# Last feed-forward of a two-layer trunk kernel: high and low token parts in one 512-column operand, down-projection in one pass

## The chip, the cores and the metric

The kernel runs on one core of a Trainium2 chip. The metric is the device time of one execution in microseconds (us); the time of a kernel is the median of its runs. The trace is one execution taken by the hardware profiler. TensorE, VectorE, ScalarE, GpSimd and SyncE are called PE, DVE, ACT, POOL and SP, as in the profile; PEld is PE's weight load. Every engine takes its own instructions in program order and waits at one whose inputs are not there.

## The reference, cut to what matters

Two layers, each a SwiGLU feed-forward, three token mixers merged by gates, and a second SwiGLU feed-forward, on 256 latent tokens (`x`) and 256 context tokens. The context is not needed after the last mixer, so the last feed-forward works on 256 tokens. In float32:

```python
def _swiglu(h, w_up, w_down):
    u, v = jnp.split(h @ w_up, 2, axis=-1)
    return (jax.nn.silu(u) * v) @ w_down
...
x = x + 0.5 * mx[8] * _swiglu(_modulate(_rmsnorm(x, norm_g[l, 2]), mx[6], mx[7]), w_ffn2_in[l], w_ffn2_out[l])
...
return _rmsnorm(x, final_g)
```

The model width is 1024 (8 tiles of 128), the hidden width 2816 (22 tiles of 128).

## The kernel before, in words

**Products.** Activations lie feature-major, `xt[k]` being 128 features by tokens. A float32 product is made of three matmuls in the fp32r format: each operand is split into a high part (a copy rounded to fp32r, on ACT) and a low part (operand minus high part, on DVE; `split`, L127), and the kernel adds high weight x high token, low weight x high token and high weight x low token into the same PSUM columns. All matmuls are recorded at L110, all ScalarE activations at L119, all two-input VectorE operations at L122 and L125 (helpers `mm`, `act`, `tt`, `stt`).

**Units.** The weights come in units (`Unit`): one DMA of up to 512 KB (4 tiles of 128 rows by 256 columns) into a ring of 6 buffers `wr`, a split into a ring of 4 pairs `wh` and `wl`, and two parts, one for each 128 output columns (m = 0 and 1). `fm_units` (L411) makes the units of a product of 256 output columns; in one of 256 tokens a part issues 12 matmuls of 256 columns: for each of the 4 tiles high x high and low x high, then 4 times high weight x low token.

**Order of the work.** The program list is walked at L1372. For each part it issues the matmuls, then calls `ahead()` (L1347), which issues loads and splits as far as the rings allow, and then what takes the part's result from PSUM. A unit is split once the unit 4 places before it has had its last matmul issued. So behind an input unit pair the order on ACT and DVE is: result of m = 0, split of a later unit, result of m = 1, then the split that follows the next unit. There is one split for each unit and one result for each part of every second unit.

**The last feed-forward** is `ffn` (L487) with n = T = 256. It works in blocks of 256 hidden columns (2 tiles): 2 units of up weights, then 2 units of gate weights. For each tile, `up` (L496) takes Silu from PSUM on ACT; `gate` (L500) multiplies by the gate product from PSUM on DVE and splits the result into two tiles of the 69-slot ring, one instruction on ACT and one on DVE. `bounds = [0, 12, KF]` cuts the hidden tiles into two passes: 6 blocks, a down-projection over 12 tiles (4 column blocks x 3 units), then 5 blocks and a down-projection over 10 tiles (4 x 3 units, the third of 2 tiles). Each pass ends for each of the 8 output tiles in `residual` (L406), one DVE instruction that adds the gated result to `xt[m]`. After the last pass `to_out` (L1209) squares the tile on ACT, adds the square on DVE, scales on DVE and lets PE transpose the tile two places before; `final` (L1226) ends the kernel.

**Its start.** `across` (L455) puts the units of the first block aside (`far`): they are split into slots of the 69-slot ring instead of `wh` and `wl`, in two halves. The first is split before the norm, the second after it, the third and the fourth when their first part is reached. `norm` (L393) makes 8 scaled tiles on DVE, 8 high tiles `hh` on ACT, then 8 low tiles `hl` on DVE. The weights of the modulation's last term (`ada`, L280: two DVE instructions for each of 8 units) are mixed into the stage, 5 of them into blocks 2 and 3.

Of the kernel before, what the change touches and what calls it, by code (L numbers as in the profile page):

```python
# [10 lines left out]
F32R = mybir.dt.float32r  # L11
U32 = mybir.dt.uint32
ACTF = mybir.ActivationFunctionType
ALU = mybir.AluOpType
# [3 lines left out]
KD = 8  # L18
T = 256
FFN = 2816  # L20
KF = FFN // 128
# [69 lines left out]
def f32(ap):  # L91
    return ap.bitcast(F32)
# [3 lines left out]
def trunk_kernel(ctx: ExitStack, tc: tile.TileContext, a: dict, out: bass.AP, dbg=None):  # L96
# [8 lines left out]
    S = Ring(sp, N_SLOT, "s")  # L105
# [3 lines left out]
    def mm(o, l, r, start=True, stop=True):  # L109
        nc.tensor.matmul(o, l, r, start=start, stop=stop)  # L110
# [7 lines left out]
    def act(o, i, f, **kw):  # L118
        nc.scalar.activation(out=o, in_=i, func=f, **kw)  # L119

    def tt(o, x, y, op):
        nc.vector.tensor_tensor(out=o, in0=x, in1=y, op=op)  # L122

    def stt(o, x, s, y, op0, op1):
        nc.vector.scalar_tensor_tensor(out=o, in0=x, scalar=s, in1=y, op0=op0, op1=op1)  # L125

    def split(src, hi, lo):  # L127
        act(hi, src, ACTF.Copy)
        tt(lo, src, f32(hi), ALU.subtract)
# [24 lines left out]
    mods = [const.tile([128, 9, KD, 2], F32, name=f"mods{l}") for l in range(DEPTH)]  # L154
# [4 lines left out]
    xt = [None] * KD  # L159
    hh = [None] * KD  # L160
    hl = [None] * KD
# [204 lines left out]
    def scale_of(c):  # L366

        if c.start == 0:
            st["r"] = S.get()
        ps = P.get()  # L370
        mm(ps[:, c], ones_d, st["sq"][:, c])
        rstd_of(ps, c, st["r"])
        P.put(ps)

    def modulate(l, ni, ss, ks):

        todo = []
        for k, s in ((k, s) for k in ks for s in ss):
            c = slice(T * s, T * s + T)
            if s == 0:  # L380
                hh[k], hl[k] = S.get(F32R), S.get(F32R)
            t, shift = S.get(), mods[l][:, 3 * ni, k, s:s + 1]
            stt(t[:, c], xt[k][:, c], mods[l][:, 3 * ni + 1, k, s:s + 1], st["r"][:, c], ALU.mult, ALU.mult)
            act(hh[k][:, c], t[:, c], ACTF.Identity, bias=shift)
            todo.append((k, c, t, shift))
        for k, c, t, shift in todo:
            stt(hl[k][:, c], t[:, c], shift, f32(hh[k][:, c]), ALU.add, ALU.subtract)
            S.put(t)

    def norm_over():  # L390
        S.put(st["r"], st["sq"])

    def norm(l, ni, s, n):  # L393
        scale_of(slice(T * s, T * s + T))
        modulate(l, ni, (s,), range(KD))
        if T * s + T == n:
            norm_over()

    def drop_h():
        for k in range(KD):  # L400
            S.put(hh[k], hl[k])

    def wblock(w, r0, nk, c0, nc_):
        return w[r0:r0 + 128 * nk, c0:c0 + nc_].rearrange("(k p) c -> p k c", p=128)

    def residual(l, i, m, c, ps):  # L406
        for s in range(c.start // T, c.stop // T):
            cs = slice(T * s, T * s + T)
            stt(xt[m][:, cs], ps[:, cs], mods[l][:, i, m, s:s + 1], xt[m][:, cs], ALU.mult, ALU.add)

    def fm_units(w, c0, width, n, done, rh=None, kd=KD, r0=0, by_stream=False, turned=0):  # L411

        rh = rh or (lambda k: (hh[k], hl[k]))
        box = {}
        units = []
        nm = (width + 127) // 128
        cols_ = [slice(0, T), slice(T, n)] if by_stream and n > T else [slice(0, n)]  # L420
        for k0 in range(0, kd, 4):
            nk = min(4, kd - k0)

            def part(m, c, k0=k0, nk=nk):
                def go(u):
                    if k0 == 0 and c.start == 0:
                        box[m] = P.get()
                    ps = box[m]
                    cs = slice(128 * m, min(128 * m + 128, width))
                    o = ps[0:cs.stop - cs.start, c]  # L430
                    for k in range(nk):
                        h = rh(k0 + k)[0]
                        mm(o, u.hi[:, k, cs], h[:, c], k0 + k == 0, False)
                        mm(o, u.lo[:, k, cs], h[:, c], False, False)
                    for k in range(nk):
                        mm(o, u.hi[:, k, cs], rh(k0 + k)[1][:, c], False, k0 + k == kd - 1)

                    def out_():
                        if by_stream == "twice":
                            done(m, ps, c)  # L440
                        elif c.stop == n:
                            done(m, ps, slice(0, n))
                        if c.stop == n:
                            P.put(ps)

                    return k0 + nk == kd and out_
                return go

            u = Unit(wblock(w, r0 + 128 * k0, nk, c0, width), (nk, width), [part(m, c) for c in cols_ for m in range(nm)])
            u.cost = nk * nm * n  # L450
            u.turned = turned
            units.append(u)
        return units
# [33 lines left out]
    def ffn(l, w_in, w_out, n, gi, after, by_stream=True):  # L487

        first, units, last = [], [], []
        bounds = [0, 12, KF]  # L490
        for p0, p1 in zip(bounds, bounds[1:]):
            gs = {}
            for b in range(p0, p1, 2):
                sil = {}

                def up(m, ps, c, sil=sil):  # L496
                    sil[m] = S.get()
                    act(sil[m][:, c], ps[:, c], ACTF.Silu)

                def gate(m, ps, c, b=b, sil=sil, gs=gs):  # L500
                    s = sil.pop(m)
                    tt(s[:, c], s[:, c], ps[:, c], ALU.mult)
                    gs[b + m] = (S.get(F32R), S.get(F32R))
                    split(s[:, c], gs[b + m][0][:, c], gs[b + m][1][:, c])
                    S.put(s)

                us = fm_units(w_in[l], 128 * b, 256, n, up, by_stream=by_stream and b == 0)
                us += fm_units(w_in[l], FFN + 128 * b, 256, n, gate, by_stream=by_stream and b == 0)
                if b == 0:
                    first = us  # L510
                else:
                    units += us
            if p1 == KF:
                units += [drop_h, exp_ln_tables]
            for cb in range(0, KD, 2):
                end = p1 == KF and cb == KD - 2

                def down(m, ps, c, cb=cb, done=p1 == KF):
                    residual(l, gi, cb + m, c, ps)
                    if done:  # L520
                        after(cb + m, c)

                us = fm_units(
                    w_out[l], 128 * cb, 256, n, down, rh=lambda k, gs=gs, p0=p0: gs[p0 + k], kd=p1 - p0, r0=128 * p0,
                    by_stream=end and "twice",
                )
                if end:
                    last = us
                else:
                    units += us  # L530

            def free(gs=gs):
                for t in gs.values():
                    S.put(*t)

            if p1 < KF:
                units.append(free)
        return first, units, last, free
# [729 lines left out]
    up, gate, up2 = f1[0][0][0:2], f1[0][0][2:4], f1[0][1][0:2]  # L1268
    firsts = [up[0], gate[0], up2[0]]
    for u in firsts:  # L1270
# [4 lines left out]
    prog += early[7:13] + [("split", up[0]), lambda: scale_of(slice(0, 2 * T))] + early[13:]  # L1275
    prog += [
        lambda: modulate(0, 0, (0, 1), range(4)), ("split", gate[0]), ("split", up2[0]),
        up[0], *late[0:8], gate[0], *late[8:],
        lambda: modulate(0, 0, (0, 1), range(4, 8)), norm_over, up2[0], up[1], gate[1], up2[1],
    ]  # L1280
    prog += mixed(f1[0][1][2:], [side_loads] + ada_of(0, (2, 4, 3, 5, 7, 6, 8)))
    prog += across(f1[0][2], [f1[0][3]], lambda s: norm(0, 1, s, N2), mx[0][0], N2)
    prog += mx[0][1]
    prog += across(mx[0][2], [mx[0][3]], lambda s: norm(0, 2, s, N2), f2[0][0], N2)
    prog += mixed(f2[0][1], ada_of(1, (1, 0, 2, 4, 3, 5, 7)))
    prog += across(f2[0][2], [f2[0][3]], lambda s: norm(1, 0, s, N2), f1[1][0], N2)
    prog += mixed(f1[1][1], ada_of(1, (6,)))
    prog += across(f1[1][2], [f1[1][3]], lambda s: norm(1, 1, s, N2), mx[1][0], N2)
# [83 lines left out]
    for p in flat:  # L1372
# [5 lines left out]
        elif p[0] == "part":  # L1378
# [3 lines left out]
            u = p[1]  # L1382
            if u.far and u.hi is None:
                part(u)
            end = p[2](u)
# [58 lines left out]
```

## Time and profile before

| what | value |
|---|---|
| median of 3 runs | 2257.07 us (2256.82 to 2258.47) |
| the profiled execution's own time | 2259.09 us |
| its span, first to last instruction | 2257.3 us |
| PE busy | 2199.2 us (97%), 12903 matmuls |
| PEld busy | 1881.6 us (83%) |
| DVE busy | 1437.4 us (64%) |
| ACT busy | 933.2 us (41%) |
| POOL busy | 143.0 us (6%) |
| chain that ended last | PE 85%, DVE 8%, ACT 4%, issue 2%, DMA 1% |
| granted PE clock, mean | 0.989 of full |

Busy time counts an engine's instructions; matmuls are pipelined, so the start-to-start distance of matmuls is a better measure of PE's pace than their recorded durations, which overlap. "Idle before" tells what ended the idle time ahead of an instruction. The chain that ended last is followed back from the last instruction. The last feed-forward fills the stretch from 2044 to 2257 us.

### The profile page before, as it was taken

The page shows a single profiled execution, that of the slowest core. Times are in us where ns is not written, and L with a number is a line of the kernel's source. Part 1 is how long each engine was busy: PE and PEld are TensorE (multiplying, and loading weights), DVE is VectorE, ACT ScalarE, POOL GpSimd, SP SyncE. Part 2 cuts the span into 40 slices and gives each one's busy share as a digit, 9 for nine tenths or more (in the row PEclk, how much of TensorE's full clock was granted, in tenths as well). Part 3 has the DMA queues.
Part 4 walks back from the last instruction along what each step waited for, and adds up shares of the span by engine and source line. Part 5 has one row for each costly group of instructions (what it writes and reads, how often), then busy time and mean ns, then how long its engine had stood idle before and what let it go on. Part 6 is the DMA issues. An engine that isn't in the chain of part 4 may idle for free.

```text
span 2257.3 us, 32367 instructions
## 1 busy us (share of the span) xinstructions
PE 2199.2 (97%) x12903; PEld 1881.6 (83%) x12903; DVE 1437.4 (64%) x2428; ACT 933.2 (41%) x1565; POOL 143.0 (6%) x154
## 2 busy tenths in 40 slices
PE   7999999998999999999999999999999899998998
PEld 5888888976887788888888898888888688998998
DVE  5677788867465564677876565333358755867655
ACT  4321223455566545432223242222344457664443
POOL 0000000232100110000000000000004220100000
PEclk9999999999999999999999999999999999999999
DMA  8566565331222223355656535333233223356652
GB/s 311 163 189 187 186 190 182 114 87 57 66 66 66 66 59 100 120 163 184 193 182 194 168 118 153 98 98 94 89 95 105 88 75 113 113 167 201 216 183 94
DMA packets 246647, 304.49 MB, mean 135 GB/s; under 512 B 12874, under 2 KB 218180, under 8 KB 246496
## 3 DMA queue, kind: packets, MB, share of 16 engines
q1 hardware_dynamic: 245472, 301.65, 43.3%
q8 instruction: 101, 1.65, 0.3%
q10 hardware_dynamic: 448, 0.59, 0.1%
q14 instruction: 50, 0.41, 0.1%
q0 software_dynamic: 576, 0.18, 0.0%
HBM read 298.19 MB, written 4.19 MB: 134 GB/s over the span
## 4 chain that ended last, share of the span: by engine, by line
PE 85%; DVE 8%; ACT 4%; issue 2%; DMA 1%; SPq 0%; POOL 0%; ACTq 0%; DVEq 0%
PE p_t L110 84%; ACT s_t L119 3%; DVE wl L122 2%; DVE s_t L122 2%; DVE s_t L125 2%; PE p_t L696 1%; ACT wh L119 1%; DMA s_t<-in_w_ada_dram 1%; DVE av_s L754 1%; DVE s_t L761 0%; DVE cv_s L834 0%; SPq L185 0%; DVE s_t L955 0%; DVE av_s L755 0%; DVE s_t L976 0%
## 5 line engine op out<-in xcount | busy, mean ns | idle before, releaser
L110 PE MATMUL p_t<-s_t,wh 128*128 128x512 f32 (+1 forms) x6152 | 1640.3, 353 | 1.4 <-ACT wh L119 1.1
L110 PEld LDWEIGHTS p_t<-s_t,wh 128*128 128x128 f32 x6152 | 1087.6, 189 | 171.0 <-issue 9.4
L110 PE MATMUL p_t<-s_t,wl 128*128 128x512 f32 (+2 forms) x3076 | 1046.5, 352 | 2.9 <-DVE wl L122 2.9
L122 DVE TENSOR_TENSOR wl<-wr,wh 128x1024 fp32r<-128x1024 f32 (+2 forms) x423 | 498.1, 1184 | 507.6 <-ACT wh L119 507.4
L119 ACT ACTIVATE wh<-wr 128x1024 fp32r<-128x1024 f32 (+2 forms) x423 | 414.9, 988 | 643.4 <-PE p_t L110 290.3
L110 PEld LDWEIGHTS p_t<-s_t,wl 128*128 128x128 f32 (+1 forms) x3076 | 582.2, 189 | 81.5 <-DVE wl L122 3.4
L119 ACT ACTIVATE s_t<-s_t 128x512 fp32r<-128x512 f32 (+5 forms) x322 | 175.1, 544 | 340.3 <-DVE s_t L122 213.4
L110 PE MATMUL p_t<-s_t,s_t 128*128 128x256 f32 (+4 forms) x2040 | 275.1, 302 | 14.6 <-ACT s_t L119 10.4
L110 PEld LDWEIGHTS p_t<-s_t,s_t 128*128 128x128 f32 (+2 forms) x2040 | 231.9, 186 | 45.1 <-ACT s_t L119 14.4
L293 DVE SCALAR_TENSOR_TENSOR s_t<-wr,sc,s_t 128x512 f32<-128x512 f32 x392 | 268.9, 745 | 0.0
L119 ACT ACTIVATE s_t<-p_t 128x512 f32<-128x512 f32 (+5 forms) x344 | 171.9, 522 | 193.4 <-PE p_t L110 102.2
L122 DVE TENSOR_TENSOR s_t<-s_t,s_t 128x512 fp32r<-128x512 f32 (+3 forms) x217 | 128.8, 594 | 114.1 <-ACT s_t L119 113.1
L563 POOL TENSOR_TENSOR s_t<-s_t,s_t 128x256 f32<-128x256 f32 x26 | 22.0, 844 | 1384.9 <-DVE s_t L122 1371.1
L122 DVE TENSOR_TENSOR s_t<-s_t,p_t 128x512 f32<-128x512 f32 (+1 forms) x144 | 84.9, 590 | 26.4 <-PE p_t L110 19.4
L110 PE MATMUL p_t<-wh,s_t 128*128 128x512 f32 x256 | 83.1, 397 | 0.5 <-ACT wh L119 0.5
L125 DVE SCALAR_TENSOR_TENSOR s_t<-s_t,mods,s_t 128x256 fp32r<-128x256 f32 (+1 forms) x176 | 70.6, 478 | 10.3 <-ACT s_t L119 10.3
L125 DVE SCALAR_TENSOR_TENSOR s_t<-p_t,mods,s_t 128x256 f32<-128x256 f32 x136 | 61.0, 478 | 21.5 <-PE p_t L110 21.3
L110 PEld LDWEIGHTS p_t<-wh,s_t 128*128 128x128 f32 x256 | 48.9, 191 | 10.9 <-ACT wh L119 0.8
L122 DVE TENSOR_TENSOR s_t<-p_t,kf 32x256 f32<-32x256 f32 (+1 forms) x130 | 54.8, 421 | 3.5 <-PE p_t L110 1.4
L110 PE MATMUL p_t<-wl,s_t 128*128 128x512 f32 x128 | 51.0, 398 | 3.1 <-DVE wl L122 3.1
L119 ACT ACTIVATE s_t<-p_t,av_s 128x512 f32<-128x512 f32 (+1 forms) x48 | 29.2, 614 | 46.9 <-DVE av_s L755 46.9
L696 PE MATMUL p_t<-kf,s_t 128*128 128x128 f32 x240 | 36.2, 282 | 8.8 <-DVE s_t L122 4.1
(104 smaller groups left out, 803.3 us busy)
## 6 DMA issues: line engine op xcount, KB each, us to landing
wr<-in_w_ffn_in_dram SPq DMA_DIRECT2D x176, 512.0 KB, 4.4
wr<-in_w_ada_dram SPq DMA_DIRECT2D x128, 512.0 KB, 4.5
wr<-in_w_mix_in_dram SPq DMA_DIRECT2D x108, 512.0 KB, 3.7
wr<-in_w_ffn_out_dram SPq DMA_DIRECT2D x80, 512.0 KB, 3.7
s_t<-in_w_ada_dram SPq DMA_DIRECT2D x32, 256.0 KB, 6.2
wr<-in_w_mix_out_dram SPq DMA_DIRECT2D x16, 512.0 KB, 3.4
wr<-in_w_ffn_out_dram SPq DMA_DIRECT2D x16, 256.0 KB, 2.8
wr<-in_w_br_a_dram SPq DMA_DIRECT2D x8, 512.0 KB, 3.5
```

The lines of the kernel that those rows point to most:

```text
L110: nc.tensor.matmul(o, l, r, start=start, stop=stop)
L119: nc.scalar.activation(out=o, in_=i, func=f, **kw)
L122: nc.vector.tensor_tensor(out=o, in0=x, in1=y, op=op)
L125: nc.vector.scalar_tensor_tensor(out=o, in0=x, scalar=s, in1=y, op0=op0, op1=op1)
L293: eng.scalar_tensor_tensor(out=o, in0=x, scalar=c, in1=o, op0=ALU.mult, op1=ALU.add)
L563: nc.gpsimd.tensor_tensor(out=q[:, 0:T], in0=q[:, 0:T], in1=r[:, 0:T], op=ALU.subtract)
L696: nc.tensor.transpose(pt[:, 128 * t:128 * t + 128], p[:, 128 * t:128 * t + 128], ident)
L754: nc.vector.tensor_reduce(out=v[:, m:m + 1], in_=ps[m][:, 0:nk], axis=AX.X, op=ALU.max)
```

## The change

The low part of a token tile lies beside its high part, in columns 256 to 511 of the same slot (`modulate`, and `gs` in `gate`). In the last feed-forward (`wide`, n = T) a tile's three matmuls become two: high weight x (high | low token) with 512 columns, and low weight x high token with 256. The two halves of the PSUM bank are then summed where the result is taken: by a copy and an addition for up and gate, and by a second DVE instruction in `residual`. The hidden tiles are worked in one pass: 11 blocks, then a down-projection over 22 tiles, 4 column blocks of 6 units (the last of 2 tiles).

```diff
-    def modulate(l, ni, ss, ks):
+    def modulate(l, ni, ss, ks, beside=False):
...
-            if s == 0:
+            if s == 0 and beside:
+                hh[k] = S.get(F32R)
+                hl[k] = hh[k][:, T:2 * T]
+            elif s == 0:
                 hh[k], hl[k] = S.get(F32R), S.get(F32R)
...
-    def residual(l, i, m, c, ps):
+    def residual(l, i, m, c, ps, wide=False):
         for s in range(c.start // T, c.stop // T):
             cs = slice(T * s, T * s + T)
             stt(xt[m][:, cs], ps[:, cs], mods[l][:, i, m, s:s + 1], xt[m][:, cs], ALU.mult, ALU.add)
+            if wide:
+                stt(xt[m][:, cs], ps[:, T:2 * T], mods[l][:, i, m, s:s + 1], xt[m][:, cs], ALU.mult, ALU.add)
...
-                    for k in range(nk):
+                    if wide:
+                        for k in range(nk):
+                            h = rh(k0 + k)[0]
+                            mm(ps, u.hi[:, k, cs], h, k0 + k == 0, False)
+                            mm(ps[:, 0:T], u.lo[:, k, cs], h[:, 0:T], False, k0 + k == kd - 1)
+                    for k in range(0 if wide else nk):
                         h = rh(k0 + k)[0]
                         mm(o, u.hi[:, k, cs], h[:, c], k0 + k == 0, False)
                         mm(o, u.lo[:, k, cs], h[:, c], False, False)
-                    for k in range(nk):
+                    for k in range(0 if wide else nk):
                         mm(o, u.hi[:, k, cs], rh(k0 + k)[1][:, c], False, k0 + k == kd - 1)
...
-        bounds = [0, 12, KF]
+        wide = n == T
+        bounds = [0, KF] if wide else [0, 12, KF]
...
                     sil[m] = S.get()
-                    act(sil[m][:, c], ps[:, c], ACTF.Silu)
+                    if wide:
+                        act(sil[m][:, c], ps[:, c], ACTF.Copy)
+                        tt(sil[m][:, c], sil[m][:, c], ps[:, T:2 * T], ALU.add)
+                        act(sil[m][:, c], sil[m][:, c], ACTF.Silu)
+                    else:
+                        act(sil[m][:, c], ps[:, c], ACTF.Silu)
...
                     s = sil.pop(m)
-                    tt(s[:, c], s[:, c], ps[:, c], ALU.mult)
-                    gs[b + m] = (S.get(F32R), S.get(F32R))
+                    if wide:
+                        act(s[:, T:2 * T], ps[:, c], ACTF.Copy)
+                        tt(s[:, T:2 * T], s[:, T:2 * T], ps[:, T:2 * T], ALU.add)
+                        tt(s[:, c], s[:, c], s[:, T:2 * T], ALU.mult)
+                        g = S.get(F32R)
+                        gs[b + m] = (g, g[:, T:2 * T])
+                    else:
+                        tt(s[:, c], s[:, c], ps[:, c], ALU.mult)
+                        gs[b + m] = (S.get(F32R), S.get(F32R))
                     split(s[:, c], gs[b + m][0][:, c], gs[b + m][1][:, c])
```

## Rows read from the trace of the kernel before

**Rows 1.** Chain that ended last, 2060 to 2258 us: start us, us, what.
```profile
2061.05 170.21 PE p_t L110 x1425
...
2232.41 6.47 PE p_t L110 x54
```
**Rows 2.** Groups by line and shape, 2061 to 2246 us (busy, mean ns | idle before).
```profile
L122 DVE TENSOR_TENSOR wl<-wr,wh 128x1024 fp32r<-128x1024 f32 x58 | 70.9, 1224 | 56.0 <-ACT wh L119 56.0
L119 ACT ACTIVATE wh<-wr 128x1024 fp32r<-128x1024 f32 x58 | 61.1, 1053 | 48.3 <-PE p_t L110 33.0 <-issue 12.4 <-DMA wr<-in_w_ffn_in_dram 2.8
...
L119 ACT ACTIVATE s_t<-s_t 128x256 fp32r<-128x256 f32 x22 | 9.2, 417 | 37.2 <-DVE s_t L122 37.2
L122 DVE TENSOR_TENSOR s_t<-s_t,p_t 128x256 f32<-128x256 f32 x22 | 9.1, 414 | 1.6 <-PE p_t L110 1.6
...
L293 DVE SCALAR_TENSOR_TENSOR s_t<-wr,sc,s_t 128x512 f32<-128x512 f32 x10 | 7.0, 744 | 0.0
```
**Rows 3.** ACT in order of time, behind a block's gate units.
```profile
2114.11 1.04 ACT L119 ACTIVATE wh<-wr 128x1024 fp32r<-128x1024 f32 x1
2116.77 0.42 ACT L119 ACTIVATE s_t<-s_t 128x256 fp32r<-128x256 f32 x1 [1.62 <-DVE s_t L122]
2117.10 1.04 ACT L119 ACTIVATE wh<-wr 128x1024 fp32r<-128x1024 f32 x1
```
**Rows 4.** DVE in order of time, the same stretch.
```profile
2115.18 1.22 DVE L122 TENSOR_TENSOR wl<-wr,wh 128x1024 fp32r<-128x1024 f32 x1 [0.53 <-ACT wh L119]
2116.33 0.41 DVE L122 TENSOR_TENSOR s_t<-s_t,p_t 128x256 f32<-128x256 f32 x1
2117.22 0.42 DVE L122 TENSOR_TENSOR s_t<-s_t,s_t 128x256 fp32r<-128x256 f32 x1 [0.48 <-ACT s_t L119]
```
**Rows 5.** Chain that ended last, 1480 to 1620 us, matmuls of 512 columns.
```profile
1479.80 140.31 PE p_t L110 x619
```
**Rows 6.** DVE in order of time, two dependent operations in a row (mixer's end).
```profile
2021.18 0.41 DVE L122 TENSOR_TENSOR s_t<-s_t,p_t 128x256 f32<-128x256 f32 x1
...
2021.63 0.42 DVE L122 TENSOR_TENSOR s_t<-s_t,s_t 128x256 f32<-128x256 f32 x1
```
**Rows 7.** PE in order of time, start of the stage.
```profile
2049.53 2.08 PE L110 MATMUL p_t<-s_t,s_t 128*128 128x256 f32 x8 [4.88 <-ACT s_t L119]
2052.16 7.04 PE L110 MATMUL p_t<-s_t,s_t 128*128 128x256 f32 x40 [0.55 <-DVE s_t L125]
2060.19 0.38 PE L110 MATMUL p_t<-s_t,s_t 128*128 128x256 f32 x1 [0.99 <-ACT s_t L119]
2061.05 3.13 PE L110 MATMUL p_t<-s_t,s_t 128*128 128x256 f32 x23 [0.47 <-DVE s_t L122]
```
**Rows 8.** ACT in order of time, start of the stage.
```profile
2054.28 1.28 ACT L119 ACT_TABLE_LOAD   x1
2057.80 0.39 ACT L119 ACTIVATE s_t<-p_t 128x256 f32<-128x256 f32 x1 [2.23 <-PE p_t L110]
...
2059.24 0.38 ACT L119 ACTIVATE s_t<-p_t 128x256 f32<-128x256 f32 x1
2059.52 1.14 ACT L119 ACTIVATE s_t<-wr 128x512 fp32r<-128x512 f32 x2
```
**Rows 9.** Windows of 1 us: PE, PEld, DVE, ACT, POOL busy, PEclk, DMA share, GB/s.
```profile
2045.00:2046.00 1.00, 0.00 (x0) 0.00 (x0) 1.00 (x3) 0.58 (x2) 0.00 (x0) 0.89 0.14 20
...
2054.00:2055.00 1.00, 1.00 (x6) 1.00 (x6) 1.00 (x4) 0.98 (x2) 0.00 (x0) 0.50 0.00 0
...
2056.00:2057.00 1.00, 1.00 (x10) 1.00 (x9) 1.00 (x2) 0.00 (x0) 0.00 (x0) 0.99 0.00 0
...
2060.00:2061.00 1.00, 0.38 (x1) 0.19 (x1) 1.00 (x3) 1.00 (x3) 0.00 (x0) 1.00 0.87 299
```
**Rows 10.** Chain that ended last, the tail: start us, us, what.
```profile
2246.55 0.50 DVE s_t L125
```

More of the change, by code (lines that the diff above doesn't have):

```diff
@@ L394, in norm, with drop_h @@
         scale_of(slice(T * s, T * s + T))
-        modulate(l, ni, (s,), range(KD))
+        modulate(l, ni, (s,), range(KD), n == T)
         if T * s + T == n:
             norm_over()
-    def drop_h():
+    def drop_h(beside=False):
         for k in range(KD):
-            S.put(hh[k], hl[k])
+            S.put(hh[k])
+            if not beside:
+                S.put(hl[k])
     def wblock(w, r0, nk, c0, nc_):
         return w[r0:r0 + 128 * nk, c0:c0 + nc_].rearrange("(k p) c -> p k c", p=128)
-    def residual(l, i, m, c, ps):
+    def residual(l, i, m, c, ps, wide=False):
         for s in range(c.start // T, c.stop // T):
@@ L409, in residual, with fm_units @@
             stt(xt[m][:, cs], ps[:, cs], mods[l][:, i, m, s:s + 1], xt[m][:, cs], ALU.mult, ALU.add)
-    def fm_units(w, c0, width, n, done, rh=None, kd=KD, r0=0, by_stream=False, turned=0):
+            if wide:
+                stt(xt[m][:, cs], ps[:, T:2 * T], mods[l][:, i, m, s:s + 1], xt[m][:, cs], ALU.mult, ALU.add)
+    def fm_units(w, c0, width, n, done, rh=None, kd=KD, r0=0, by_stream=False, turned=0, wide=False):
         rh = rh or (lambda k: (hh[k], hl[k]))
@@ L497, in up @@
                     sil[m] = S.get()
-                    act(sil[m][:, c], ps[:, c], ACTF.Silu)
+                    if wide:
[4 more added lines that the diff above has]
+                        act(sil[m][:, c], ps[:, c], ACTF.Silu)
                 def gate(m, ps, c, b=b, sil=sil, gs=gs):
                     s = sil.pop(m)
-                    tt(s[:, c], s[:, c], ps[:, c], ALU.mult)
-                    gs[b + m] = (S.get(F32R), S.get(F32R))
+                    if wide:
[7 more added lines that the diff above has]
+                        gs[b + m] = (S.get(F32R), S.get(F32R))
                     split(s[:, c], gs[b + m][0][:, c], gs[b + m][1][:, c])
                     S.put(s)
-                us = fm_units(w_in[l], 128 * b, 256, n, up, by_stream=by_stream and b == 0)
-                us += fm_units(w_in[l], FFN + 128 * b, 256, n, gate, by_stream=by_stream and b == 0)
+                us = fm_units(w_in[l], 128 * b, 256, n, up, by_stream=by_stream and b == 0, wide=wide)
+                us += fm_units(w_in[l], FFN + 128 * b, 256, n, gate, by_stream=by_stream and b == 0, wide=wide)
                 if b == 0:
@@ L513, in ffn @@
             if p1 == KF:
-                units += [drop_h, exp_ln_tables]
+                units += [lambda: drop_h(wide), exp_ln_tables]
             for cb in range(0, KD, 2):
@@ L518, in down @@
                 def down(m, ps, c, cb=cb, done=p1 == KF):
-                    residual(l, gi, cb + m, c, ps)
+                    residual(l, gi, cb + m, c, ps, wide)
                     if done:
@@ L524, in ffn @@
                     w_out[l], 128 * cb, 256, n, down, rh=lambda k, gs=gs, p0=p0: gs[p0 + k], kd=p1 - p0, r0=128 * p0,
-                    by_stream=end and "twice",
+                    by_stream=end and "twice", wide=wide,
                 )
@@ L533, in free @@
                 for t in gs.values():
-                    S.put(*t)
+                    S.put(*t[0:1 if wide else 2])
             if p1 < KF:
```

## Prediction

> **What bounds the kernel now.** I read the chain that ended last, then the groups by line and shape, then the queues of ACT and DVE in order of time, and last the start and the tail. From 2061.05 the chain is 170 us of matmuls and nothing else [rows 1]: PE sets the pace, and 54 matmuls in 6.47 us make 0.1198 us each. Behind it the groups show ACT waiting 33.0 us for PE before weight splits [rows 2]: ACT has time to spare. But the same group view shows a second thing: in front of 22 high parts of the gated tiles ACT stood 37.2 us waiting for DVE, 1.7 each, and DVE stood 56 us waiting for ACT's `wh`. In time order the reason is seen. Behind a gate tile the two engines hand work back and forth and neither runs ahead: `wh` on ACT at 2114.11, `wl` on DVE at 2115.18, the product at 2116.33, its high part on ACT at 2116.77, the next `wh` at 2117.10 [rows 3, 4]. The round takes 1.07 + 1.15 + 0.44 + 0.33 = 2.99 us, and none of it waits for PE. Before the change only the two gate tiles of a block run it; the two up tiles' Silu is on ACT alone. A block of 4 units costs PE 96 x 0.1198 = 11.50 us, so it is covered.
>
> **The matmuls.** 44 up and gate tiles x 8 and 8 output tiles x 22 make 528 triples. A 512-column matmul in a stretch of nothing else takes 140.31 / 619 = 0.2267 us [rows 5]. A triple goes from 3 x 0.1198 = 0.3594 to 0.2267 + 0.1198 = 0.3465: 0.0129 saved, 6.8 us in all. No row shows the two shapes alternating. The bounds: nothing saved if the narrow one takes longer behind the wide one, 13 us if the overhead of both were gone; I take the two rows' sum, since both carry the same 13 ns over their streaming time (107 and 213 ns at 2.4 GHz). The Trainium skill (TensorE: Matmul & The Clock Gate, "Back-to-back issue gap") gives 262 and 518 cycles for 256 and 512 columns when warm, 109 and 216 ns; by it the triple would save 2.6 ns and the whole 1.4 us. The rows disagree, both being 11 ns longer, and the rows are used.
>
> **Taking results out.** An up tile now needs a copy on ACT, an addition on DVE, Silu on ACT. The copy (0.39, like the Silu from PSUM [rows 8]) lies under `wl`. The addition has the product's shape (414 ns [rows 2]) and Silu now reads the slot, like the high part (417). So an up tile runs the same round as a gate tile: 2.99 us where now Silu needs no DVE. A gate tile gets one more DVE operation that depends on the last; two such operations start 0.45 apart [rows 6], so its round is 3.44. Each of the four results of a block stands in program order behind one weight split, so a block costs the pair of engines 2 x 2.99 + 2 x 3.44 = 12.86 us, while PE needs 32 x 0.3465 = 11.09. **The pair becomes the bound**, by 1.77 us for each of the 10 blocks behind the first: 17.7 us. To it comes what else is in the two queues: 5 pairs of `ada` operations (744 ns each [rows 2], 1.4 us a pair); behind an up tile they lie under Silu and the next `wh`, behind a gate tile (2 of 5) they hold the next `wl` by 0.8, so 1.6; and the load of the exp/ln tables behind the last gate, 1.28. Against it stands the lead: a unit is split when PE finishes the unit 4 places before, in about 2.3 us (1.07 + 1.23), and used 3 units later, 3 x 2.77 = 8.3; 6.0 us of delay cost nothing. Loss: 17.7 + 1.6 + 1.3 - 6.0 = 14.6 us, all in PE's waits for `wl` from about the fourth block to the first units of the down-projection. There the splits come without results and cost DVE 1.2 us against 2.77 of PE, so PE is the bound again.
>
> **One pass.** The same 24 loads of the down weights, and the same 16 additions to `xt` (8 tiles x 2 halves instead of 8 x 2 passes), each under matmuls but the last. What moves: the 12 down units of the first pass, in which ACT and DVE catch up today, no longer stand between blocks 6 and 7, so the lead is not refilled. Fewer slots are held (22 instead of up to 24 for `gs`, 8 instead of 16 for `hh` and `hl`). The loads are released by splits in the same order on SP's queue; one wait of 2.8 us for a load exists now [rows 2].
>
> **The start.** PE begins at 2049.53 with high tiles alone and gets on at 2052.16 with the first low tile [rows 7]. The wide matmul needs both at once, so everything starts at 2052.16; `norm` issues the same instructions. The clock is at 1.2 GHz until 2056.0 [rows 9]: 5.8 triples at 0.66, then 6.2 at 0.3465, and the first up tile is done at 2058.3, where Silu started at 2057.80 [rows 8]. Then, in queue order: copy 0.41; the table load 1.28, which now stands ahead of the waiting Silu before PE is done [rows 8] and comes behind the copy, since a copy did not need it; Silu 0.33; ring `wh` and `wl` 1.07 + 1.15; the second tile's addition 0.44 and Silu 0.33; the halves of the third unit's weights, 0.66 and 0.73. PE is back in full stride at about 2064.7 against 2061.05 [rows 7]: +3.6. If the load stays ahead of the copy, 0.9 less.
>
> That leaves PE without matmuls for some 4.2 us from 2059.7. In the stop of 4.9 us before 2049.53 the clock fell to half and came back at 2056.0; in the stop of 1.9 us to 2061.05 it stayed at full [rows 7, 9]. The new stop is nearer to the longer one: I take a fall, about 5 us of dense matmuls at half speed, +2.5 (bounds 0 and 3.3, half of the 6.5 us between 2049.53 and 2056.0).
>
> **The tail.** Behind the last matmuls `residual` stands twice on the path (for tiles 6 and 7), each longer by one operation of 0.50 [rows 10] that depends on the one before: +1.0.
>
> **Sum**: -6.8 + 14.6 + 3.6 + 2.5 + 1.0 = +14.9 us, on 2259.09 for the profiled execution 2274.0; the median of the runs lies 2.0 below that execution, so **2272.0**.
>
> **Rivals.** (1) *The round keeps up.* Place: ACT and DVE in blocks 2 to 11. It decides at 11.09 us a block: if the copy and addition of an up tile overlapped the weight split, as Silu does now, a block would cost the pair some 10 us and PE would stay the bound. Then -6.8 + 3.6 + 1.0 = -2.2 us: 2254.9, and with a start that costs only 1 us 2252.3. For it: ACT is busy 41% and DVE 64% of the span. Against it: the queue is in order, and the four handoffs of the gate round are there in the rows with no gap that PE ends. Were the skill's pair of gaps right, the matmuls would save only 1.4 and this rival would give 2260. (2) *Loads run late*: `ada` units hold load buffers until DVE reaches them, now up to 10 us later; one landing of 4 to 5 us exposed once or twice more on the pair's path gives 2277 to 2280. For it, the one wait of 2.8 us today; against it, slower splits need loads less often. (3) *The wide pair saves nothing*: PE would need 11.50 a block, the pair still binds, 10 x 1.36 + 2.9 - 6.3 = 10.2 in place of 14.6 - 6.8: 2274; hardly told apart by time, but by the distance of matmuls.
>
> **How the numbers follow.** What a measurement of this kernel can tell from no change is about 0.2%, 4.5 us. The pair as the bound has 0.78, with loads late on top 0.10, the round keeping up 0.12, of which a third ends over 0.2% faster. Slower 0.88, same 0.08, faster 0.04. The range: rounds 0.2 us shorter (40 of them, -8) and no fall of the clock (-2.5) give 2261.5; 0.05 longer for two more handoffs in each round (+4) and a late load (+4) give 2280.
>
> **What would show it.** PE's idle time before matmuls with `wl` or `wh`, ended by DVE `wl`, now 0, should come to about 15 us, in waits of 0.4 to 0.9 each unit from the fourth block on; ACT should hold no waits for PE before `wh` in that stretch and wait for DVE before 44 Silu and high parts. Two matmuls of 512 and 256 columns should take 0.347 together. At the start PE should pass 2064 before full stride, with the table load behind the first copy. If PE's chain is unbroken from there to the tail, the forecast is wrong.

## The result, and the profile after

The changed kernel takes **2273.78 us** (median of 4 runs, 2273.48 to 2275.28); the kernel before, run beside it, 2257.77 (4 runs). The ratio is 1.0068, 95% interval 1.0055 to 1.0081: 16 us slower. The profiled execution took 2275.28 us, its span 2273.5, against 2259.09 and 2257.3 before.

The page's first and fourth part (busy us, share and instructions of each engine; chain by engine):

```profile
PE 2199.4 (97%) x12375; PEld 1853.8 (82%) x12375; DVE 1453.5 (64%) x2472; ACT 943.8 (42%) x1609; POOL 144.2 (6%) x154
...
PE 82%; DVE 10%; ACT 5%; issue 2%; DMA 1%; SPq 0%; POOL 0%; ACTq 0%; DVEq 0%
```

PE has 528 matmuls fewer (one for each *triple*: the three matmuls that one 128x128 tile of weights took before, now a pair of 512 and 256 columns) and is busy as long as before; DVE and ACT have 16 and 11 us more work. None of this tells 16 us of loss. The chain does: PE's share of it fell from 85% to 82%, and where it was 170 us of matmuls without a break [rows 1], it now reads (chain that ended last; start us, us, what):

```profile
2052.48 6.29 PE p_t L110 x24
...
2064.46 30.64 PE p_t L110 x159
...
2110.95 21.94 PE p_t L110 x120
2132.89 1.03 ACT wh L119
...
2135.86 1.05 ACT wh L119
2136.94 1.23 DVE wl L122
2138.53 0.43 DVE s_t L122
2139.31 1.05 ACT wh L119
...
2210.94 18.77 PE p_t L110 x107
```

PE sets the pace only where the chain shows it in long pieces. From 2132.89 to 2210.94 it is nearly all ACT and DVE, in the order `wh`, `wl`, addition, `wh`, though PE's first wait for them in this stretch comes only at 2167.43. ACT in order of time, one block of that stretch:

```profile
2135.86 1.04 ACT L119 ACTIVATE wh<-wr 128x1024 fp32r<-128x1024 f32 x1
2136.81 0.36 ACT L119 ACTIVATE s_t<-p_t 128x256 f32<-128x256 f32 x1
2138.99 0.42 ACT L119 ACTIVATE s_t<-s_t 128x256 fp32r<-128x256 f32 x1 [1.81 <-DVE s_t L122]
2139.31 1.04 ACT L119 ACTIVATE wh<-wr 128x1024 fp32r<-128x1024 f32 x1
...
2142.76 1.04 ACT L119 ACTIVATE wh<-wr 128x1024 fp32r<-128x1024 f32 x1
...
2145.43 0.42 ACT L119 ACTIVATE s_t<-s_t 128x256 f32<-128x256 f32 x1 [1.36 <-DVE s_t L122]
2145.75 1.04 ACT L119 ACTIVATE wh<-wr 128x1024 fp32r<-128x1024 f32 x1
...
2148.74 1.04 ACT L119 ACTIVATE wh<-wr 128x1024 fp32r<-128x1024 f32 x1
```

The distance from one `wh` to the next is the round: 3.45 us twice behind a gate tile, 2.99 twice behind an up tile, 12.88 for the block. ACT is idle for 1.81 and 1.36 us of each, and cannot use it: the `wh` of the next unit stands behind a Silu or a high part that waits for DVE, and DVE's next work, `wl`, waits for that `wh`. Neither is short of time: from 2133 to 2211 us ACT is busy for 41 and DVE for 47 of 78 us (window: PE, PEld, DVE, ACT, POOL busy, PEclk, DMA share, GB/s):

```profile
2133.00:2211.00 78.00, 73.73 (x402) 60.99 (x400) 47.35 (x72) 41.34 (x73) 0.00 (x0) 1.00 0.51 159
```

The groups from 2061 to 2262 us say it in sums (busy, mean ns | idle before):

```profile
L110 PEld LDWEIGHTS p_t<-s_t,wl 128*128 128x128 f32 x495 | 94.1, 190 | 7.6 <-DVE wl L122 7.5
...
L119 ACT ACTIVATE wh<-wr 128x1024 fp32r<-128x1024 f32 x59 | 61.6, 1046 | 11.2 <-PE p_t L110 8.5 <-issue 2.7
...
L119 ACT ACTIVATE s_t<-s_t 128x256 f32<-128x256 f32 x27 | 11.3, 418 | 43.3 <-DVE s_t L122 30.0 <-DVE s_t L125 13.2
...
L119 ACT ACTIVATE s_t<-s_t 128x256 fp32r<-128x256 f32 x22 | 9.2, 418 | 39.0 <-DVE s_t L122 39.0
```

ACT's wait for PE before `wh` fell from 33.0 us [rows 2] to 8.5, all in the down-projection (from 2064 to 2208 us it is 0.0); new is the wait of Silu for DVE. PE's own waits from 2040 to 2270 (us in total, times, longest; those of the tail and one of 1.5 us ahead of the stage left out):

```profile
PE p_t L110 <- DVE s_t L125: 7.5, 1, 7.5
PE p_t L110 <- ACT s_t L119: 4.3, 1, 4.3
PE p_t L110 <- DVE s_t L293: 4.1, 1, 4.1
PE p_t L110 <- DVE wl L122: 3.5, 8, 0.8
...
PE p_t L110 <- ACT wh L119: 0.8, 1, 0.8
```

The first is the wait for the norm (4.88 + 0.55 before, with 2.08 us of matmuls of high tiles between [rows 7], now in one piece), the second the new stop behind the first two units. The third is one that I had not listed: PE standing at the 16 `pick` matmuls of the `ada` sum (small matmuls that add up the last modulation term), which are in PE's queue, for a DVE operation that the rounds had delayed. PE in order of time there, and windows of 2 us around it (PE, PEld, DVE, ACT, POOL busy, PEclk, DMA share, GB/s):

```profile
2106.02 0.28 PE L110 MATMUL p_t<-s_t,wl 128*128 128x256 f32 x1
2110.38 1.20 PE L110 MATMUL p_t<-s_t,pick 128*32 128x128 f32 x16 [4.08 <-DVE s_t L293]
```
```profile
2110.00:2112.00 2.00, 1.47 (x17) 0.86 (x18) 1.90 (x3) 1.24 (x3) 0.00 (x0) 0.76 0.68 183
2112.00:2114.00 2.00, 2.00 (x7) 1.65 (x7) 1.41 (x4) 0.95 (x2) 0.00 (x0) 0.50 0.91 266
2114.00:2116.00 2.00, 2.00 (x12) 1.74 (x11) 1.55 (x2) 0.68 (x2) 0.00 (x0) 0.89 1.06 354
```

Behind the stop the granted clock stands at 0.50 (1.2 GHz) for about 3.4 us. The start, ACT in order of time, and a window:

```profile
2058.79 0.38 ACT L119 ACTIVATE s_t<-p_t 128x256 f32<-128x256 f32 x1 [4.15 <-PE p_t L110]
2059.19 1.28 ACT L119 ACT_TABLE_LOAD   x1
...
2063.47 0.42 ACT L119 ACTIVATE s_t<-s_t 128x256 f32<-128x256 f32 x1 [1.35 <-DVE s_t L122]
2063.79 1.14 ACT L119 ACTIVATE s_t<-wr 128x512 fp32r<-128x512 f32 x2
```
```profile
2064.00:2070.00 6.00, 5.54 (x16) 4.43 (x17) 3.72 (x5) 2.92 (x5) 0.00 (x0) 0.50 0.71 213
```

The table load stands behind the first copy, the third unit's halves come last, PE is back at 2064.46 and at half clock until 2070.0.

**Where 16 us went.** Start: 2064.46 for 2061.05, 3.4, of which 0.3 came from ahead of the stage (the norm's first matmuls stand at 2044.27 for 2043.95). Half clock on 5.54 us of matmuls: 2.8. Picks: a wait of 4.1, and 1.6 for the clock behind it (the shares missing in three windows of 2 us: 0.48 + 1.00 + 0.22, a little of it idle). Rounds: the 78.05 us from 2132.89 hold 200 triples, which take PE about 69.9 (88 up to 2163.8 at 0.3533, the others near 0.3467): 8.2. Of these, 2.1 are PE's waits for `wh` and `wl` at the first triple of the down-projection, whose split stands on ACT behind the load of the exp/ln tables (1.28 us from 2207.28). Tail: from PE's last product to the end 11.8 us for 10.8: 1.0. Matmuls: about 280 triples at 0.3467 instead of 0.3594, 230 at 0.3533: 5.0 saved. 3.4 + 2.8 + 5.7 + 8.2 + 1.0 - 5.0 = 16.1; the spans differ by 16.2.

### The profile page after: what moved, and what is told of

It reads as the page before. It is cut to its first block, busy times and chain, and to the rows that moved or that the text cites. A ratio compares the mean times of both kernels' runs of the same rounds, so it can differ in the third digit from the quotient of the medians.

```text
span 2273.5 us, 31401 instructions
## 1 busy us (share of the span) xinstructions
PE 2199.4 (97%) x12375; PEld 1853.8 (82%) x12375; DVE 1453.5 (64%) x2472; ACT 943.8 (42%) x1609; POOL 144.2 (6%) x154
## 4 chain that ended last, share of the span: by engine, by line
PE 82%; DVE 10%; ACT 5%; issue 2%; DMA 1%; SPq 0%; POOL 0%; ACTq 0%; DVEq 0%
PE p_t L110 80%; DVE wl L122 3%; DVE s_t L122 3%; ACT s_t L119 3%; ACT wh L119 2%; DVE s_t L125 2%; PE p_t L723 1%; DMA s_t<-in_w_ada_dram 1%; DVE av_s L781 1%; DVE s_t L788 0%; DVE s_t L293 0%; DVE cv_s L861 0%; SPq L185 0%; DVE s_t L982 0%; DVE av_s L782 0%
## 5 line engine op out<-in xcount | busy, mean ns | idle before, releaser
L110 PEld LDWEIGHTS p_t<-s_t,wh 128*128 128x128 f32 x5656 | 1025.5, 189 | 193.2 <-issue 9.4
L110 PE MATMUL p_t<-s_t,wl 128*128 128x512 f32 (+2 forms) x3076 | 1062.9, 352 | 6.4 <-DVE wl L122 6.4
L122 DVE TENSOR_TENSOR wl<-wr,wh 128x1024 fp32r<-128x1024 f32 (+2 forms) x423 | 498.0, 1185 | 498.8 <-ACT wh L119 498.3
L119 ACT ACTIVATE s_t<-s_t 128x512 fp32r<-128x512 f32 (+5 forms) x344 | 184.3, 536 | 380.9 <-DVE s_t L122 245.3
L119 ACT ACTIVATE s_t<-p_t 128x512 f32<-128x512 f32 (+5 forms) x366 | 179.8, 512 | 198.0 <-PE p_t L110 107.3
L122 DVE TENSOR_TENSOR s_t<-s_t,s_t 128x512 fp32r<-128x512 f32 (+3 forms) x217 | 128.9, 594 | 113.9 <-ACT s_t L119 112.9
L122 DVE TENSOR_TENSOR s_t<-s_t,p_t 128x512 f32<-128x512 f32 (+1 forms) x166 | 94.2, 567 | 30.0 <-PE p_t L110 17.9
L125 DVE SCALAR_TENSOR_TENSOR s_t<-s_t,mods,s_t 128x256 fp32r<-128x256 f32 (+1 forms) x176 | 70.7, 478 | 10.3 <-ACT s_t L119 10.3
L122 DVE TENSOR_TENSOR s_t<-p_t,kf 32x256 f32<-32x256 f32 (+1 forms) x130 | 54.8, 421 | 3.5 <-PE p_t L110 1.4
```

## The experiments

Theory: ACT and DVE's round is the bound because each result holds the next split in two queues. Rivals: the added work itself is too much for the two engines; the single pass costs the lead; the 512-column operand is at fault. Except where a kernel is said to leave something out, all compute the whole product.

**One pass alone.** Tokens side by side and one pass, but three matmuls of 256 columns and the results taken as before:

```diff
-                            mm(ps, u.hi[:, k, cs], h, k0 + k == 0, False)
-                            mm(ps[:, 0:T], u.lo[:, k, cs], h[:, 0:T], False, k0 + k == kd - 1)
-                    for k in range(0 if wide else nk):
+                    for k in range(nk):
                         h = rh(k0 + k)[0]
                         mm(o, u.hi[:, k, cs], h[:, c], k0 + k == 0, False)
...
-                        act(sil[m][:, c], ps[:, c], ACTF.Copy)
-                        tt(sil[m][:, c], sil[m][:, c], ps[:, T:2 * T], ALU.add)
-                        act(sil[m][:, c], sil[m][:, c], ACTF.Silu)
-                    else:
+                    if True:
                         act(sil[m][:, c], ps[:, c], ACTF.Silu)
...
```

> The layout and the single pass of the change, but three matmuls of 256 columns again and no sums. Handoff theory: a block's rounds are those of before (two of 2.99, the up tiles beside them), PE needs 11.50 and bounds: same as the kernel before, 2256 to 2259. If the single pass or the side-by-side slots cost: 2265 or more.

Measured: 2259.42 against 2258.98, ratio 1.0003 (0.9994 to 1.0013). The layout and the single pass cost nothing that can be told; the loss is in the wide matmul and what it asks for.

**Two passes, wide.** `bounds = [0, 12, KF]` again, all else of the change kept.

> The changed kernel with the hidden tiles in two passes again (12 and 10), all else as changed. Handoff theory (a block costs ACT and DVE 12.86 us in rounds, PE 11.09): the 12 down units between blocks 6 and 7 refill the lead of 6.0 us, so 5 x 1.77 + 1.6 - 6.0 = 4.5 in the first pass and 5 x 1.77 + 1.3 - 6.0 = 4.1 in the second, 8.6 in place of 14.6: 6 us below the changed kernel, about 2268, still about 10 above the kernel before. If the single pass as such were the cost: back to 2258 or below. If the matmuls or the start were the cost: no change, 2274.

Measured: 2274.77, ratio 1.0069 (1.0052 to 1.0085): no gain, a miss. The waits before `wl` are gone as expected, that of 4.1 us at the picks is not, and PE waits elsewhere (PE in order of time; its waits for DVE from 2228 to 2240 are two more of the kind):

```profile
2141.44 0.28 PE L110 MATMUL p_t<-s_t,wl 128*128 128x256 f32 x1
2143.20 0.50 PE L110 MATMUL p_t<-s_t,wh 128*128 128x512 f32 x1 [1.48 <-DVE s_t L122]
...
2234.04 0.50 PE L110 MATMUL p_t<-s_t,wh 128*128 128x512 f32 x1 [0.88 <-DVE s_t L122]
...
2237.49 0.79 PE L110 MATMUL p_t<-s_t,wh 128*128 128x512 f32 x1 [2.83 <-DVE s_t L122]
```

It waits for the low part of the last gated tiles. At a pass's end two units (5.5 us) stand between the last gate and the unit that needs its tiles; in one pass five (13.9 us). So one pass hides at its end what it loses in the middle, and "the lead is not refilled" was no loss by itself.

**The sums left out.** Up and gate read columns 0 to 255 alone (the product of high weight and low token is left out of both):

```diff
-                        act(sil[m][:, c], ps[:, c], ACTF.Copy)
-                        tt(sil[m][:, c], sil[m][:, c], ps[:, T:2 * T], ALU.add)
-                        act(sil[m][:, c], sil[m][:, c], ACTF.Silu)
-                    else:
+                    if True:
                         act(sil[m][:, c], ps[:, c], ACTF.Silu)
...
-                        act(s[:, T:2 * T], ps[:, c], ACTF.Copy)
-                        tt(s[:, T:2 * T], s[:, T:2 * T], ps[:, T:2 * T], ALU.add)
-                        tt(s[:, c], s[:, c], s[:, T:2 * T], ALU.mult)
+                        tt(s[:, c], s[:, c], ps[:, c], ALU.mult)
```

> The changed kernel, but up and gate take only columns 0 to 255 of the PSUM bank: the products of high weight and low token of the up and gate projections are computed and left out of the result; no copy and no addition there. Handoff theory: rounds as before, PE bounds at 11.09 a block; what is left is the saving of 6.8 in matmuls, about 1.0 at the tail and 1 at the start: 2252 to 2254. If the wide pair saves nothing: 2258 to 2260. If the matmuls were the cost: 2270.

Measured: 2256.49 against 2258.98, ratio 0.9987 (0.9978 to 0.9997): the loss goes with the sums. The time is above what was expected; from about 2103 on a triple took 0.3533 and not 0.3467. PE at the start (order of time):

```profile
2060.90 0.49 PE L110 MATMUL p_t<-s_t,s_t 128*128 128x512 f32 x1 [0.99 <-ACT s_t L119]
2061.78 4.43 PE L110 MATMUL p_t<-s_t,s_t 128*128 128x256 f32 x24 [0.39 <-DVE s_t L122]
```

No long stop, and no fall of the clock behind it.

**The same work, in another order.** This parts the order of the round from the amount of work: the same instructions, but Silu and the split of the gated tile are issued one part later, behind the next weight split.

```diff
-                        act(sil[m][:, c], sil[m][:, c], ACTF.Silu)
+                        t = sil[m]
+                        soon.append((n_part + 1, lambda: act(t[:, c], t[:, c], ACTF.Silu)))
...
-                    split(s[:, c], gs[b + m][0][:, c], gs[b + m][1][:, c])
-                    S.put(s)
...
+                    def rest(g=gs[b + m]):
+                        split(s[:, c], g[0][:, c], g[1][:, c])
+                        S.put(s)
...
+                        soon.append((n_part + 1, rest))
```

> The same instructions on every engine as in the changed kernel, but Silu of an up tile and the split of a gate tile are issued one part later, behind the next weight split, so no engine stands at an operation whose input is still being made. Handoff theory: the order costs, not the amount; ACT needs some 7 us and DVE some 8 to 9 of a block's 11.09, the 14.6 us go and about 1 us at the start: 2257 to 2260, and PE's waits for wl in the blocks are 0. If DVE or ACT were simply overloaded, or the matmuls were slow: 2270 or more.

Measured: 2258.96 against 2258.98, ratio 1.0002 (0.9992 to 1.0011): the 16 us are gone by order alone. The waits before `wl` and at the picks are gone, a stop of 2.7 us at the start is left, and behind it PE's chain is unbroken up to the tail (chain; groups from 2061 to 2246):

```profile
2065.07 150.53 PE p_t L110 x859
```
```profile
L110 PEld LDWEIGHTS p_t<-s_t,wl 128*128 128x128 f32 x491 | 92.6, 189 | 0.0
...
L119 ACT ACTIVATE s_t<-s_t 128x256 fp32r<-128x256 f32 x22 | 9.1, 414 | 15.1 <-DVE s_t L122 14.9
```

ACT's wait before the high parts fell from 39.0 to 15.1 us. The two engines had the time; what they lacked was work that could start.

**One more step in the gate's round**, as a dose of the suspected cost: an operation that changes no value, between product and split.

```diff
                         tt(s[:, c], s[:, c], s[:, T:2 * T], ALU.mult)
+                        tt(s[:, c], s[:, c], s[:, c], ALU.max)
```

> The changed kernel with one more DVE operation in each gate round (the maximum of the product with itself, same result), dependent on the one before. Handoff theory: 0.45 more in 2 rounds of each of 10 blocks: 9.0 above the changed kernel, 2282 to 2284, and a block in the saturated stretch takes 13.8 in place of 12.9. If matmuls or loads set the pace there: 2274.

Measured: 2285.41 (one run). ACT's `wh` in order of time:

```profile
2140.46 1.04 ACT L119 ACTIVATE wh<-wr 128x1024 fp32r<-128x1024 f32 x1
...
2144.37 1.04 ACT L119 ACTIVATE wh<-wr 128x1024 fp32r<-128x1024 f32 x1
...
2148.28 1.05 ACT L119 ACTIVATE wh<-wr 128x1024 fp32r<-128x1024 f32 x1
...
2151.27 1.04 ACT L119 ACTIVATE wh<-wr 128x1024 fp32r<-128x1024 f32 x1
```

Gate rounds 3.91 (+0.46), up rounds 2.99: 13.80 a block. The time is 26.3 us over the kernel before that ran beside it (2259.08), where the changed kernel was 16.0 over: 10.3 us for 22 operations of 0.45, together 9.9 us, so nearly all of these lie on the path. Of the 10.3, 1.7 are a longer wait at the picks (5.8 for 4.1), and a part belongs to the clock: behind that wait it stands at half until about 2118, in the changed kernel until 2114.4.

**Two passes with the results later.**

> Two passes again, as in two_passes, but with Silu and the gate split issued one part later, as in results_later. That run lost its regained lead at the two pass ends, where PE stood for gated tiles that were still in the queues of ACT and DVE (2140 to 2143 and 2230 to 2239 us). Handoff theory: without the rounds the results are not late, PE's waits for DVE at both pass ends are under 1 us together, and the time is that of results_later, 2257 to 2261. If a pass end costs by itself: 2265 or more.

Measured: 2262.64 (one run; the kernel before, run beside it, 2259.08), a little above what was expected. PE's waits for DVE `s_t` L122 are 1.7 us, 1.5 of them ahead of the stage; the waits at the ends of the passes are gone, so those were the same late round.

**The start too.** Results later, and the third and fourth unit split and the Silu table loaded ahead of the first matmuls; then, besides, the picks some 29 units later.

```diff
-... [("split", u), lambda: norm_of(0), ("split", after[1])]
+... [("split", u), lambda: ahead(), lambda: norm_of(0), *(("split", v) for v in after[1:]), silu_table]
```

> results_later, and at the start the weights of the third and fourth unit are split before the first parts instead of behind the first up tiles, and the Silu table is loaded there by a one-column Silu. If the start costs as forecast (PE's stop behind the second unit, in results_later 2.7 us, and some 2 us for the half clock that follows it), both go: 2253 to 2255, with the clock at full from 2058 on. If the stop is hidden anyway: 2259.

> far_both, and the 16 small matmuls that sum the last modulation term are issued some 29 units later, just before the down-projection. In no_sums and results_later the pair of 512 and 256 columns took 0.3467 us up to these matmuls at about 2103 and 0.3533 behind them. If such an interruption sets the pace: 0.3467 up to the down-projection, some 290 triples by 6.6 ns, 1.9 us less: 2251 to 2253. If the pace has another cause: as far_both.

Measured: 2253.85, ratio 0.9977 (0.9968 to 0.9987), and 2253.48, ratio 0.9976 (0.9966 to 0.9985). PE's chain starts with the first unit and has no break up to the tail (chain of the first, then of the second):

```profile
2053.60 158.27 PE p_t L110 x892
```
```profile
2052.82 155.37 PE p_t L110 x892
```

The 2.9 us between these two are not the picks' place alone: the first execution ran at 0.3533 a triple from its start on, the second at 0.3467 up to its picks near 2178 (some 350 triples, 2.3 us), and the clock was back at full 5.6 us behind the first matmul in the first and 4.3 in the second. The medians do not differ: the 1.9 us that were expected of the picks' place did not come.

**The same start for the kernel before.**

> The kernel before, with the third and fourth unit's halves split ahead of the first matmuls and the Silu table loaded there, as in far_both; nothing of the change. The gain of far_both (5 us against the kernel before) can come from the start alone or from the wide matmuls with it. If from the start alone: this kernel gives about 2254 too. If the wide matmuls count: the only stop here is the one of 1.9 us to 2061.05, it goes, and 2256.5 to 2257.5 is left, some 3 us over far_both.

Measured: 2257.33 against 2259.62, ratio 0.9989 (0.9980 to 0.9998), 2.3 us; the stop to 2061.05 is gone (the chain has 177.06 us of matmuls from 2051.98 on). The two kernels below, which have the wide matmuls with the same start, ran beside it and took 2253.48 and 2254.33: the 3 to 4 us between, by difference, belong to the wide matmuls (5.0 saved above, less 1.0 at the tail).

**The last two tiles narrow**, to give back what `residual` put on the tail.

```diff
-                    residual(l, gi, cb + m, c, ps, wide)
+                    residual(l, gi, cb + m, c, ps, wide and cb < KD - 2)
```

> far_both_picks with the last two output tiles by narrow matmuls (44 triples) and one residual operation each, so that the two operations of 0.50 us that the change put on the tail go. Theory: the tail is 1.0 shorter, 44 triples cost 0.3 to 0.6 more: 0.4 to 0.7 us under far_both_picks, 2252.8 to 2253.1, and in the trace the time from PE's last product to the end is 10.8 instead of 11.8. Rival: the second operation lay under other work at the tail, and the time is 0.3 to 0.6 longer.

Measured: 2253.48, ratio 0.9974 (0.9965 to 0.9984). From PE's last product (2242.10) to the end (2252.8) it is 10.7 us, for 12.0 in the kernel that it was made from; in the time the gain cannot be told.

**The order of widths.** Four matmuls of 512 columns, then four of 256.

> far_both_picks with a part's matmuls in another order: the four of 512 columns in a row, then the four of 256, instead of alternating. Two paces of the pair of 512 and 256 columns were seen, 0.3467 and 0.3533. If the alternation of widths makes the slower one, a part of four triples takes 4 x 0.3467 = 1.387 us everywhere and the time is 1 to 2 us under far_both_picks. If the pace belongs to something else (the state of the engine after an interruption), both paces show again and the time is that of far_both_picks within 0.5 us.

Measured: 2254.33, ratio 0.9975 (0.9964 to 0.9985). PE in order of time:

```profile
2064.77 1.09 PE L110 MATMUL p_t<-s_t,wh 128*128 128x512 f32 x4
2065.70 0.64 PE L110 MATMUL p_t<-s_t,wl 128*128 128x256 f32 x4
2066.17 1.09 PE L110 MATMUL p_t<-s_t,wh 128*128 128x512 f32 x4
```

A part takes 1.40 us, 0.351 a triple, also at 2141 and 2215: neither of the two paces, and neither of the two outcomes expected. In one execution, this settles nothing.

## Why the prediction was right, and where not

Forecast 2272.0, measured 2273.78; by profiled executions +14.9 and +16.2.

**Right: the round as the bound.** 2.99 and 3.44 were forecast for the rounds, 2.99 and 3.45 measured, 12.88 a block for 12.86. That this sets the time is shown from both sides: the same instructions in another order lose nothing against the kernel before, and one more dependent step costs 10 us more (one run). The rival that the round keeps up falls, but what it described is what the reordered kernel does.

**Right in the sum, wrong in the place.** 14.6 us were forecast for the rounds, "all in PE's waits for `wl`", 0.4 to 0.9 each from the fourth block on, with none of ACT's for PE before `wh` (0.0 there, as said). Waits for `wl` or `wh` were recorded for 4.3 us only, and the first stands at 2167.43, at the end of the ninth block; by the distance of matmuls 8.2 are lost there, and 4.1 + 1.6 at the picks, behind the fourth block. The step that failed: the `ada` operations were costed as a delay of DVE's queue, without asking who waits for them. PE does, at the picks, and everything behind stands. While it stood, ACT and DVE went on and won back lead (behind it the chain has 21.94 us of matmuls without a break), so the sum (13.9) hardly changed. That it comes so near to 14.6 is in part luck: 1.6 of it is a second fall of the clock, which the forecast had put at nothing.

**Half right: the matmuls.** 6.8 us were forecast, about 5.0 came. The sum of the two rows [rows 5] gives 0.3465 and a triple does take 0.3467:

```profile
2073.09 0.28 PE L110 MATMUL p_t<-s_t,wl 128*128 128x256 f32 x1
...
2077.94 0.28 PE L110 MATMUL p_t<-s_t,wl 128*128 128x256 f32 x1
```

(14 triples in 4.85 us) but in nearly half of the stage it takes 0.3533, where 0.0061 is saved instead of 0.0129. From the gaps of single matmuls in the Trainium skill (TensorE: Matmul & The Clock Gate, "Back-to-back issue gap") the estimate for the pair is 0.325; no row shows that.

**Right: the start and the clock.** Full stride was forecast for 2064.7, with the load behind the copy, as it came; PE began again at 2064.46 with the high half of the weights and went on with the low half at 2065.18. 2.5 were forecast for the clock, 2.8 measured. (The stop of 1.9 us that the forecast compares with is two waits, 0.99 and 0.47, with a matmul between them [rows 7].) **Right: the tail**, 1.0.

**Rivals.** No load was late on the path: ACT's idle time before `wh` names no DMA any more, where 2.8 us of it did [rows 2]. That the wide pair saves nothing falls with 0.3467.

**One pass.** "The lead is not refilled" was named as what moves; the run with two passes shows that refilling it gains nothing, as the late results then come due sooner.

## What to carry to other kernels

Before an operation is added to a result's path, look at what stands behind it in each in-order queue: here 0.4 us operations cost some 14 us on engines that were busy for 41 and 47 of 78 us there, since each held the next weight split, and issuing the same operations one part later gave it back. Cost a round by its dependent steps, not by its busy time, and ask of every operation that it delays who waits for that one, on PE's queue too. A wider operand saves little when the matmuls are already dense (5 us of 190 here), so its price elsewhere decides.

## What the runs showed that had not been expected

- The pair of 512 and 256 columns has two paces at full clock, 0.3467 and 0.3533 us, which change at interruptions of PE (picks, transposes, waits) and hold for tens of us; an execution can also run the second from its start. With widths grouped it took 0.351. The cause is open.
- During or just behind stops of PE of 4.3, 4.1, 2.8 and 2.7 us the granted clock fell to half; at the one of 1.48 us with two passes it did not, nor at the two short waits near 2060 with one matmul between them, before the change and with the sums left out (0.99 and about 0.4 us each). The stop of 2.7 us is that of the reordered kernel (the window of 2 us behind it, columns as above):

```profile
2066.00:2068.00 2.00, 2.00 (x8) 1.71 (x7) 1.91 (x3) 1.10 (x3) 0.00 (x0) 0.50 0.51 153
```
